# Keys and queries of a hybrid layer's mixer as one wide seven-product projection, with the mixer's steps in another order

## The chip, the cores and the metric

The kernel runs on one core of a Trainium2 chip. The metric is the device time of one execution in microseconds (us). TensorE multiplies, VectorE (DVE) and ScalarE (ACT) prepare its operands and empty its accumulators in PSUM, GpSimd (POOL) does a little elementwise work and issues some transfers, SyncE (SP) issues the transfers of the weights.

## The reference

One layer of a hybrid decoder on 256 tokens of width 2048, all in float32: a half feed-forward block, a mixer, a second half feed-forward block, a final norm.

```python
def rmsnorm(x, g):
    return x * rsqrt(mean(x * x, -1) + EPS) * g

def layer(h):
    h = h + 0.5 * swiglu(rmsnorm(h, ffn1_norm), ffn1_w_in, ffn1_w_out)
    u = rmsnorm(h, mix_norm) @ w_in_mix        # columns: pool 1024 | q 512 | k 512 | v 1024 | gate 1024 | rank 16
    y_pool = pool_mixer(u[..., :1024], w_pool, pool_scale)
    y_gla = gla_mixer(q, k, v, gate, rank, w_alpha, b_alpha, gla_norm)
    h = h + concat([y_pool, y_gla], -1) @ w_out_mix
    h = h + 0.5 * swiglu(rmsnorm(h, ffn2_norm), ffn2_w_in, ffn2_w_out)
    return rmsnorm(h, final_norm)

def swiglu(h, w_in, w_out):                    # w_in: 2048 x 11264, w_out: 5632 x 2048
    gate, up = split(h @ w_in, 2, -1)
    return (silu(gate) * up) @ w_out
```

The pooling mixer takes means over the last 2, 4, 8 or 16 tokens (four groups of 256 channels), minus the token, through a 256x256 matrix for each group. The other one is gated linear attention with four heads in chunks of 64 tokens: the decay is the log-sigmoid of `rank @ w_alpha + b_alpha`, divided by 16 and summed along the chunk; keys and queries are scaled by its exponentials; the output of each head is normalised by its own root mean square and multiplied by silu of the gate columns.

## The kernel before

Tokens are two row tiles of 128 (`t`). Activations are kept transposed, 16 k-tiles of 128 channels by 256 tokens, split into a high and a low part (`hT1`); they are TensorE's stationary operand. Weights stream past them, up to 512 columns to a matmul. Each product is made of three matmuls, high by high, low by high and high by low (`three`, L198 to L202), so almost every matmul in the trace has line L202.

**Weights.** `load` (L142) brings 128 x 2048 numbers through SP's queue into one of a few raw buffers. ScalarE rounds them to the high part (L166), VectorE subtracts that to get the low part (L167). The results lie in a ring of blocks of 512 columns (16 blocks, six more in the feed-forward stages). The blocks are taken in turn; where a run of blocks crosses the ring's end, its split is cut in two.

**Two kinds of step.** A step covers two k-tiles (a pair, `kp`) by 1024 columns. A plain step (S, `s_step`) is 8 products, 24 matmuls, from four ring blocks. A seven-product step (W, `w_step`, after Strassen and Winograd) is 21 matmuls, from seven blocks. For it VectorE also takes differences of the raw weights (`less`, L190) and makes four sums of the activations for each pair (`s_factors`, L416, L442, and the split L153/L154). Four of the seven products go into four PSUM banks of their own (`pw`), which `combine` (L326 to L330) adds up at the end of a group. `Group` keeps a group of steps in PSUM; `wide` runs one in the mixer, with hooks called after given steps. `W_MIX` lists the pairs that are W steps in the mixer.

**PSUM and SBUF.** The pool `psy` has two buffers of two banks, `ps_t` has four banks, for `pw` and everything small. In SBUF the dictionary `homes` gives a name to each place of the mixer; names that share a place follow one another.

**Order of the mixer.** `finish1` ends FFN 1, and between its transposes runs the first halves of two `project` calls: the last 336 gate columns with 16 rank columns (`w_mgr`), and the keys (`w_mk`). Then come the rest of these two, the rank rows (`r_sb`, transposed to `rT`, L799 to L802), the values `mv` (a wide group, steps SSWWWWSS, with `decay` as a hook: `z`, L817, its Abs, Exp and Ln, `la`, L824, and the exponentials `E1`, `E2`, `Es`), `keys`, the queries `mq` (`project`), the pooling columns `mp` (wide, with `state` and `scores` as hooks), `attend` (o, its squares `sq_o`, the roots `ro_r` through POOL at L366, the scalings L962), `pool(0)` and gate columns `mg0`, `pool(1)` and `mg1`, then the output projection `h2` in two halves, in which `gate_y` multiplies y by the gates and transposes it (`tp_y`). The sums of `h2` with `h_mid`, loaded by POOL's queue, are at L1086; the instructions of the first sums are kept in `cleared`.

Each engine runs its instructions in one fixed order, and a waiting instruction holds back all behind it on its engine. A scheduler lays these orders out when the program is built, from the data flow and its own costs; it may move an instruction across steps where its operands allow. `issue_after` binds it: what its block issues on the engine of the named instruction comes behind that instruction there, in order only, without a wait for its end.

Of the kernel before, what the change touches and what calls it, by code (L numbers as in the profile page):

```python
# [28 lines left out]
F32 = mybir.dt.float32  # L29
# [54 lines left out]
W_MIX = (0, 1, 2, 3)  # L84
# [4 lines left out]
def layer(ctx: ExitStack, tc: tile.TileContext, io):  # L89
# [94 lines left out]
    def w_step(src):  # L184
# [11 lines left out]
        f.update(zip(("T1", "T3", "T2", "T4"), parts_of(w, PAIRS)))  # L196
# [503 lines left out]

    kd = list(range(KD))
    hact = act_of(*hT1)
    early = []

    def finish1(np_, grp, h):
# [27 lines left out]
    ps_r, ps_k = early  # L733
# [75 lines left out]
    E1 = block([P, HEADS, T], F32, "E1")  # L809
    E2 = gpool.tile([P, HEADS, T], F32, tag="g_lo", name="E2")  # L810
    Es = gpool.tile([P, HEADS * DK], F32, tag="g_lo", name="Es")

    def decay(_):
        z = []
        for t in range(NT):
# [3 lines left out]
            z.append(zt)  # L819
# [454 lines left out]
```

## Time and profile before

| | before |
|---|---|
| median of 3 runs | 1695.22 us (1694.63 to 1695.98) |
| profiled execution, its own time | 1695.91 us |
| its span (first to last instruction) | 1694.1 us, granted clock 0.998 |
| VectorE busy, share of the span | 1517.9 us, 90% |
| ScalarE busy, share of the span | 1028.1 us, 61% |
| mixer: first matmul of `mgr` | 702.9 us |
| mixer: first transpose of y | 908.9 us |

In lines of the profile an operation stands as output<-inputs, with names of the program without their numbers; "128x512" is partitions by elements. In a timeline, the first number is the start from the beginning of the span, the second the duration, both in us. In a group line, "x32 | 12.7, 396 | 0.0" is the count, the busy time in us, the mean of one in ns, and the engine's idle time before them with what ended it.

### The profile page before, as it was taken

What the parts mean: (1) busy time and instruction counts of PE and PEld (TensorE: products, weight loads), DVE (VectorE), ACT (ScalarE), POOL (GpSimd) and SP (SyncE); (2) the same over time, 40 slices, a digit from 0 to 9 for tenths busy, and PEclk for the clock granted to TensorE, in tenths of its full rate; (3) what the DMA queues carried; (4) which work ended last, traced back from release to release, by engine and by line L of the source; (5) the groups of instructions that cost most, each with busy time, mean ns of one, the idle gap of its engine ahead of it and who ended that gap; (6) DMA issues with size and microseconds to landing.
All of it is one profiled execution on the core that took longest, in us unless ns stands there. A gap on an engine that the chain in (4) does not pass through costs nothing.

```text
span 1694.1 us, 20977 instructions
## 1 busy us (share of the span) xinstructions
PE 1678.6 (99%) x7654; PEld 1392.0 (82%) x7654; DVE 1517.9 (90%) x1709; ACT 1028.1 (61%) x1309; POOL 58.1 (3%) x69
## 2 busy tenths in 40 slices
PE   9999999999999999999999999999999999999997
PEld 6888888888888888887898888888888888888876
DVE  8899999999999996777867888999999999999987
ACT  7665665665665664557565665656656656656554
POOL 0000000000000000000000000000000000000001
PEclk9999999999999999999999999999999999999999
DMA  9766766866866777546466584666767667677772
GB/s 344 281 183 234 247 185 230 257 170 228 261 183 219 257 213 252 211 140 229 166 208 204 169 318 141 205 232 201 214 229 226 207 225 227 196 235 227 218 275 75
DMA packets 106330, 369.50 MB, mean 218 GB/s; under 512 B 11873, under 2 KB 15073, under 8 KB 106226
## 3 DMA queue, kind: packets, MB, share of 16 engines
q1 hardware_dynamic: 97026, 335.63, 58.4%
q0 software_dynamic: 8480, 31.46, 8.7%
q8 instruction: 60, 0.98, 0.2%
q10 hardware_dynamic: 720, 1.07, 0.2%
q14 instruction: 44, 0.36, 0.1%
HBM read 340.85 MB, written 27.26 MB: 217 GB/s over the span
## 4 chain that ended last, share of the span: by engine, by line
PE 90%; DVE 5%; DMA 3%; issue 2%; ACT 1%; SPq 0%; ACTq 0%; DVEq 0%
PE ps_zi L202 15%; PE ps_fi L202 15%; PE ps_zo L202 14%; PE ps_fo L202 13%; PE pw_zi L202 8%; PE pw_fi L202 8%; PE ps_h L202 3%; DVE ring_lo L167 3%; PE ps_mg L202 2%; PE ps_mp L202 2%; PE ps_mv L202 2%; DMA ring_raw<-in_ffn_w_in 2%; PE pw L202 1%; PE ps_w_mk L202 1%; PE ps_mq L202 1%
## 5 line engine op out<-in xcount | busy, mean ns | idle before, releaser
L166 ACT CAST ring_hi<-ring_raw 128x1024 fp32r<-128x1024 f32 (+2 forms) x947 | 843.0, 930 | 525.3 <-DMA ring_raw<-in_ffn_w_in 109.8
L167 DVE TENSOR_TENSOR ring_lo<-ring_raw,ring_hi 128x1024 fp32r<-128x1024 f32 (+5 forms) x797 | 969.2, 1244 | 112.1 <-ACT ring_hi L166 110.9
L190 DVE TENSOR_TENSOR ring_raw<-ring_raw 128x1024 f32<-128x1024 f32 (+1 forms) x381 | 324.3, 863 | 2.6 <-DMA ring_raw<-in_ffn_w_in 2.1
L202 PE MATMUL ps_fi<-ring_hi,xT_hi 128*128 128x512 f32 x368 | 141.4, 390 | 2.4 <-ACT ring_hi L166 2.4
L202 PE MATMUL ps_fi<-ring_lo,xT_hi 128*128 128x512 f32 x368 | 143.4, 390 | 0.2 <-DVE ring_lo L167 0.2
L202 PE MATMUL ps_fi<-ring_hi,xT_lo 128*128 128x512 f32 x368 | 143.2, 389 | 0.0
L202 PE MATMUL ps_zi<-ring_lo,h_hi 128*128 128x512 f32 x362 | 141.2, 390 | 0.1
L202 PE MATMUL ps_zi<-ring_hi,h_lo 128*128 128x512 f32 x362 | 139.7, 390 | 0.0
L202 PE MATMUL ps_zi<-ring_hi,h_hi 128*128 128x512 f32 x362 | 139.4, 390 | 0.0
L202 PE MATMUL ps_fo<-ring_lo,fhi 128*128 128x512 f32 x352 | 138.2, 393 | 0.3 <-DVE ring_lo L167 0.3
L202 PE MATMUL ps_fo<-ring_hi,flo 128*128 128x512 f32 x352 | 137.8, 391 | 0.0
L202 PE MATMUL ps_fo<-ring_hi,fhi 128*128 128x512 f32 x352 | 135.9, 391 | 0.0
L202 PE MATMUL ps_zo<-ring_lo,zhi 128*128 128x512 f32 x338 | 131.9, 390 | 1.2 <-DVE ring_lo L167 1.2
L202 PE MATMUL ps_zo<-ring_hi,zlo 128*128 128x512 f32 x338 | 131.7, 391 | 0.0
L202 PE MATMUL ps_zo<-ring_hi,zhi 128*128 128x512 f32 x338 | 131.6, 394 | 0.0
L202 PE MATMUL pw_zi<-ring_hi,s_z 128*128 128x512 f32 x342 | 117.6, 389 | 0.1
L202 PE MATMUL pw_fi<-ring_hi,s_f 128*128 128x512 f32 x336 | 116.1, 390 | 0.3 <-ACT ring_hi L166 0.3
L202 PEld LDWEIGHTS ps_fi<-ring_hi,xT_hi 128*128 128x128 f32 x368 | 69.0, 188 | 17.5 <-ACT ring_hi L166 3.4
L202 PEld LDWEIGHTS ps_fi<-ring_lo,xT_hi 128*128 128x128 f32 x368 | 69.1, 188 | 15.1 <-DVE ring_lo L167 0.8
L202 PEld LDWEIGHTS ps_fi<-ring_hi,xT_lo 128*128 128x128 f32 x368 | 69.1, 188 | 14.3
L202 PEld LDWEIGHTS ps_zi<-ring_lo,h_hi 128*128 128x128 f32 x362 | 68.0, 188 | 14.5 <-DVE ring_lo L167 0.6
L202 PEld LDWEIGHTS ps_zi<-ring_hi,h_hi 128*128 128x128 f32 x362 | 68.0, 188 | 14.1
(353 smaller groups left out, 2597.1 us busy)
## 6 DMA issues: line engine op xcount, KB each, us to landing
ring_raw<-in_ffn_w_in SPq DMA_DIRECT2D x350, 512.0 KB, 5.4
ring_raw<-in_ffn_w_out SPq DMA_DIRECT2D x176, 512.0 KB, 5.7
ring_raw<-in_w_out_mix SPq DMA_DIRECT2D x32, 512.0 KB, 4.9
hd<-half_f POOLq DMA_DIRECT2D x18, 512.0 KB, 8.4
hd<-half_z POOLq DMA_DIRECT2D x18, 512.0 KB, 7.8
ring_raw<-in_w_mv SPq DMA_DIRECT2D x16, 512.0 KB, 4.3
ring_raw<-in_w_mp SPq DMA_DIRECT2D x16, 512.0 KB, 4.9
ring_raw<-in_w_mg SPq DMA_DIRECT2D x16, 352.0 KB, 3.5
```

Of the source, the lines that this page charges most:

```text
L166: nc.scalar.copy(out=hi[:, j:k, :], in_=src[:, i + j : i + k, :])
L167: nc.vector.tensor_tensor(out=lo, in0=src[:, i : i + n, :], in1=hi.bitcast(F32), op=ALU.subtract)
L190: nc.vector.tensor_tensor(out=out, in0=x, in1=y, op=ALU.subtract)
L202: nc.tensor.matmul(ps, x, y, start=start and i == 0, stop=stop and i == 2, **kw)
```

## The change

Keys and queries become one wide group, `mkq`, of 1024 columns (`w_mkq` holds both), in pair order 0, 1, 2, 5, 3, 4, 6, 7, with W steps for pairs 4, 5 and 6. Its first two steps stand in `finish1`, where the first halves of the two projections stood. `W_MIX` is now the pairs 4 to 7, for all three wide groups. The order behind it is new: the whole of `mgr`, the pooling columns `mp` (hooks after its second step: `turn_r` and `decay`), `mg0` in two halves with `decay2` and `heads_in` (keys and queries turned and scaled), the values `mv` (hook: `scores`), `state` and `pool(0)`, and `mg1`, with `attend` and `pool(1)` after its first half; `load_h(0)` and `load_h(1)` follow. `decay` is cut in two, and `la` is now a minimum for each row tile and one subtraction for both. High and low parts of the pooling weights, `band`, `v` and `up` have other homes. Four places order instructions of W steps: behind `made_r` (the rank rows), step 2 of `mp`; behind `cleared[0]`, the low parts of step 2, and behind `cleared[1]`, step 3, both in the second half of `h2`, where step 3 stood behind `cleared[0]`.

```diff
-W_MIX = (0, 1, 2, 3)
+W_MIX = (4, 5, 6, 7)
...
-    def w_step(src):
+    def w_step(src, behind=None):
...
-        f.update(zip(("T1", "T3", "T2", "T4"), parts_of(w, PAIRS)))
+        with tc.issue_after(behind) if behind else nullcontext():
+            f.update(zip(("T1", "T3", "T2", "T4"), parts_of(w, PAIRS)))
...
+    def wide_group(name, order, w_kps, adds):
+        kinds = "".join("W" if kp in w_kps else "S" for kp in order)
+        return Group({"y": psy}, ("y",), kinds, name, ones=four_banks, adds=adds, calm=True)
...
-    early = []
+    heads = []
+    heads_order = (0, 1, 2, 5, 3, 4, 6, 7)
...
             if np_ == 1:
-                w, cw = (("w_mgr", 336), ("w_mk", CW))[n % 2]
-                early.append(project(hact, kd, io[w], cw, w, part=slice(0, KD // 2)))
+                if not heads:
+                    heads.append(wide_group("mkq", heads_order, (4, 5, 6), lambda: heads_adds))
+                kp = heads_order[n % 2]
+                heads[0].s(half_steps(hact, kp), s_step(io["w_mkq"][kp]))
             transposed_rows(
...
-    def wide(act, src, order, w_kps, s_in, name, adds, hooks={}, behind={}):
...
+    def wide(act, src, order, w_kps, s_in, name, adds, hooks={}, grp=None, behind={}, low_behind={}):
+        grp = grp or wide_group(name, order, w_kps, lambda: adds)
+        kinds = grp.kinds
         for i, kp in enumerate(order):
+            if i < grp.n:
+                continue
             if kinds[i] == "W":
                 with tc.issue_after(behind[i]) if i in behind else nullcontext():
-                    b = w_step(src[kp])
+                    b = w_step(src[kp], low_behind.get(i))
                 grp.w(half_steps(act, kp), s_in[kp], b)
             else:
                 grp.s(half_steps(act, kp), s_step(src[kp]))
...
+    h_make = s_factors(pair_of(*hT1), W_MIX, "mix", (("h", "h0"), ("h", "h1")))
+    h_in = {kp: h_make(kp) for kp in W_MIX}
...
+    heads_adds = [block([P, 2, CW], F32, f"mkq_add{t}") for t in range(NT)]
...
-    gw = (352, 352, 336 - RANK)
-    ps = project(hact, kd, io["w_mgr"], gw[2] + RANK, "mgr", ps_r, slice(KD // 2, KD))
+    grp = wide(hact, io["w_mkq"], heads_order, (4, 5, 6), h_in, "mkq", None, grp=heads[0])
+    out_of(grp, kq)
+    k_sb, q_sb = ([kq[t][:, n * CW : (n + 1) * CW] for t in range(NT)] for n in range(2))
+    ps = project(hact, kd, io["w_mgr"], gw[2] + RANK, "mgr")
...
+    r_sb = small.tile([P, NT, RANK], F32, tag="r_sb", name="r_sb")
     for t in range(NT):
-        r_sb = small.tile([P, RANK], F32, tag="r_sb", name=f"r_sb{t}")
-        nc.vector.tensor_scalar_mul(r_sb, ps[t][:, gw[2] : gw[2] + RANK], rs(t))
-        tp = ps_t.tile([P, CW], F32, tag="tp", name=f"tp_r{t}")
-        nc.tensor.transpose(tp[:RANK, :P], r_sb, ident)
-        nc.vector.tensor_copy(rT[:RANK, t * P : (t + 1) * P], tp[:RANK, :P])
+        made_r = nc.vector.tensor_scalar_mul(r_sb[:, t, :], ps[t][:, gw[2] : gw[2] + RANK], rs(t)).ins
         nc.scalar.activation(
             out=gsil[t][:, gw[0] + gw[1] :], in_=ps[t][:, : gw[2]], func=AF.Silu, scale=rs(t)
         )
...
+    z = []
+    def turn_r(_):
+        tp = ps_t.tile([P, CW], F32, tag="tp", name="tp_r")
+        for t in range(NT):
+            nc.tensor.transpose(tp[:RANK, t * P : (t + 1) * P], r_sb[:, t, :], ident)
+        nc.vector.tensor_copy(rT[:RANK, :], tp[:RANK, :T])
     def decay(_):
-        z = []
         for t in range(NT):
             zt = ps_t.tile([P, CW], F32, tag="tp", name=f"z{t}")
             nc.tensor.matmul(zt, rT[:, t * P : (t + 1) * P], walpha, start=True, stop=True)
             nc.scalar.activation(out=e[:, t, :], in_=zt, func=AF.Abs)
-            z.append(zt)
+            nc.vector.tensor_scalar(
+                out=la[:, t, :], in0=zt, scalar1=0.0, scalar2=None, op0=ALU.min
+            )
         nc.scalar.activation(out=e, in_=e, func=AF.Exp, scale=-1.0)
         nc.scalar.activation(out=e, in_=e, func=AF.Ln, bias=1.0)
-        for t in range(NT):
-            nc.vector.scalar_tensor_tensor(
-                out=la[:, t, :], in0=z[t], scalar=0.0, in1=e[:, t, :], op0=ALU.min, op1=ALU.subtract
-            )
+        nc.vector.tensor_tensor(out=la, in0=la, in1=e, op=ALU.subtract)
+    def decay2(_):
@@ -844,11 +879,7 @@
         nc.scalar.activation(out=Es, in_=sf, func=AF.Exp)
-    ps = project(hact, kd, io["w_mk"], CW, "mk", ps_k, slice(KD // 2, KD))
-    k_sb = gpool.tile([P, NT, HEADS * DK], F32, tag="g_hi", name="k_sb")
...
         for s, tp in headsT(k_sb, "k"):
             nc.vector.tensor_tensor(out=kiT[:, s, :], in0=tp, in1=E2[:, s, :], op=ALU.mult)
...
-    mix_order = [kp for kp in range(KD // 2) if kp not in W_MIX]
-    mix_order = mix_order[:2] + list(W_MIX) + mix_order[2:]
...
+    mix_order = (0, 1, 4, 5, 6, 7, 2, 3)
+    pool_order = (0, 1, 4, 5, 2, 6, 7, 3)
+    def gate_cols(c, hooks={}):
+        c0 = c * gw[0]
+        ps = None
+        for i in range(2):
+            ps = project(hact, kd, io["w_mg"][c], gw[c], f"mg{c}", ps, slice(i * KD // 2, (i + 1) * KD // 2))
+            if i in hooks:
+                hooks[i](None)
...
+    adds = [block([P, 2, CW], F32, f"mp_add{t}") for t in range(NT)]
+    out_of(wide(hact, io["w_mp"], pool_order, W_MIX, h_in, "mp", adds, behind={2: made_r}, hooks={1: lambda _: (turn_r(None), decay(None))}), up)
+    def heads_in(_):
+        keys()
...
-    out_of(wide(hact, io["w_mv"], mix_order, W_MIX, h_in, "mv", adds, {5: decay}), v)
-    keys()
-    ps = project(hact, kd, io["w_mq"], CW, "mq")
-    q_sb = gpool.tile([P, NT, HEADS * DK], F32, tag="g_lo", name="q_sb")
...
-    for s, tp in headsT(q_sb, "q"):
...
+    gate_cols(0, {0: decay2, 1: heads_in})
...
-    adds = [block([P, 2, CW], F32, f"mp_add{t}") for t in range(NT)]
-    grp = wide(hact, io["w_mp"], mix_order, W_MIX, h_in, "mp", adds, {0: state, 5: scores})
-    up = hpool.tile([P, NT, 2 * CW], F32, tag="h1", name="up")
...
-    out_of(grp, up)
-    attend(None)
+    v = hpool.tile([P, NT, HEADS * DV], F32, tag="h1", name="v")
...
+    adds = [block([P, 2, CW], F32, f"mv_add{t}") for t in range(NT)]
+    out_of(wide(hact, io["w_mv"], mix_order, W_MIX, h_in, "mv", adds, {6: scores}), v)
...
-    load_h(0)
...
-        wp_hi, wp_lo = (block([P, 2, 2, DV], F32R, f"wp_{x}{i}") for x in ("hi", "lo"))
+        if True:
+            both = hpool.tile([P, 2, 2 * CW], F32R, tag="h0", name=f"wp{i}s")
+            wp_hi, wp_lo = (both[:, x].rearrange("p (j c d) -> p j c d", j=2, c=2) for x in range(2))
         split_to(wp_hi, wp_lo, wp)
...
-    for c in range(2):
-        pool(c)
-        c0 = c * gw[0]
-        ps = project(hact, kd, io["w_mg"][c], gw[c], f"mg{c}")
...
+    (state(None), pool(0))
+    gate_cols(1, {0: lambda _: (attend(None), pool(1))})
+    load_h(0)
     load_h(1)
...
-        grp = wide(yact, io["w_out_mix"][np_], out_order[np_], W_OUT if np_ else (), y_in, f"h2{np_}", adds, hooks[np_], behind={3: cleared[0]} if np_ else {})
+        grp = wide(yact, io["w_out_mix"][np_], out_order[np_], W_OUT if np_ else (), y_in, f"h2{np_}", adds, hooks[np_], behind={3: cleared[1]} if np_ else {}, low_behind={2: cleared[0]} if np_ else {})
```

What this does to the order of instructions shows at three places. On TensorE, before, in the value projection (`ps_mv`, `pw`) at the first matmul of `decay`:

```order
L202 MATMUL pw_5419<-ring_lo,s_mix_5321 128x512
L202 MATMUL pw_5419<-ring_hi,s_mix_5321 128x512
L817 MATMUL z_5549<-walpha,rT 128x512
L202 MATMUL pw_5418<-ring_lo,s_mix_5321 128x512
L202 MATMUL pw_5418<-ring_hi,s_mix_5321 128x512
```

And after, in the pooling projection (`ps_mp`):

```order
L203 MATMUL ps_mp_5486<-ring_hi,s_mix_5094 128x512
L203 MATMUL ps_mp_5486<-ring_hi,h_hi_127 128x512
L851 MATMUL z_5552<-walpha,rT 128x512
L851 MATMUL z_5556<-walpha,rT 128x512
L203 MATMUL pw_5576<-ring_hi,h_hi_127 128x512
```

Before, the second of the two stood 53 rows further on; now they are neighbours.

On VectorE, at the end of the last chunk of FFN 2's first product, before (`add_zi` are the combining sums, `ps_zi` the sum with the plain part, `ring_lo` splits of weights):

```order
L327 TENSOR_TENSOR add_zi_1_11575<-pw_zi_0_11377,add_zi_0_11574 128x512
L328 TENSOR_TENSOR add_zi_0_11574<-pw_zi_1_11378,add_zi_1_11575 128x512
L329 TENSOR_TENSOR add_zi_1_11575<-pw_zi_1_11378,add_zi_1_11575 128x512
L519 TENSOR_TENSOR ps_zi_0_11362<-ps_zi_0_11362,add_zi_0_11574 128x1024
L167 TENSOR_TENSOR ring_lo<-ring_raw,ring_hi 128x2048
L330 TENSOR_TENSOR add_zi_1_11575<-pw_zi_1_11378,add_zi_1_11575 128x512
L167 TENSOR_TENSOR ring_lo<-ring_raw,ring_hi 128x2048
```

And after:

```order
L167 TENSOR_TENSOR ring_lo<-ring_raw,ring_hi 128x1024
L328 TENSOR_TENSOR add_zi_1_11598<-pw_zi_0_11400,add_zi_0_11597 128x512
L167 TENSOR_TENSOR ring_lo<-ring_raw,ring_hi 128x2048
L329 TENSOR_TENSOR add_zi_0_11597<-pw_zi_1_11401,add_zi_1_11598 128x512
L330 TENSOR_TENSOR add_zi_1_11598<-pw_zi_1_11401,add_zi_1_11598 128x512
L167 TENSOR_TENSOR ring_lo<-ring_raw,ring_hi 128x2048
L520 TENSOR_TENSOR ps_zi_0_11385<-ps_zi_0_11385,add_zi_0_11597 128x1024
L167 TENSOR_TENSOR ring_lo<-ring_raw,ring_hi 128x1024
L331 TENSOR_TENSOR add_zi_1_11598<-pw_zi_1_11401,add_zi_1_11598 128x512
```

The same five sums now have splits between them, one of them ahead of the second sum and one ahead of the 1024-wide one.

On ScalarE, from the last square of the first row tile's o to the scalings of the second one's, before (`ring_hi` casts here are gate weights, `wp_hi` pooling weights):

```order
L379 ACTIVATE sq_o_6116,so_6103<-o_1_6107 128x256
L166 CAST ring_hi<-ring_raw 128x2x352
L962 ACTIVATE y_g_hi<-o_0_6104,ro_r 128x256 x2
L962 ACTIVATE y_g_hi<-o_1_6107,ro_r 128x256 x2
L379 ACTIVATE sq_o_6143,so_6132<-o_0_6133 128x256
L379 ACTIVATE sq_o_6145,so_6132<-o_0_6133 128x256
L379 ACTIVATE sq_o_6147,so_6132<-o_1_6138 128x256
L153 CAST wp_hi_6172<-wp_6167 128x1024
L379 ACTIVATE sq_o_6149,so_6132<-o_1_6138 128x256
L166 CAST ring_hi<-ring_raw 128x2x352 x3
L962 ACTIVATE y_g_lo<-o_0_6133,ro_r 128x256 x2
```

And after, from the split of the pooling weights to the scalings of the second row tile (`ring_hi` casts are output weights, `p_hi` the pooled rows, `gsil` the gates):

```order
L153 CAST wp1s<-wp_6441 128x1024
L380 ACTIVATE sq_o_6419,so_6408<-o_0_6409 128x256
L380 ACTIVATE sq_o_6421,so_6408<-o_0_6409 128x256
L166 CAST ring_hi<-ring_raw 128x1024
L380 ACTIVATE sq_o_6423,so_6408<-o_1_6414 128x256
L380 ACTIVATE sq_o_6425,so_6408<-o_1_6414 128x256
L153 CAST p_hi_6451<-pp_0_6453 128x512
L166 CAST ring_hi<-ring_raw 128x512
L914 ACTIVATE gsil_5140<-ps_mg_6318,r_h_r 128x352
L914 ACTIVATE gsil_5141<-ps_mg_6318,r_h_r 128x352
L988 ACTIVATE y_g_lo<-o_0_6409,ro_r 128x256 x2
```

The squares and scalings of the attention now share ScalarE's queue with the pooling of `pool(1)`, the last gates and the first output weights.

More of the change, by code (lines that the diff above doesn't have):

```diff
@@ L699, in project, with four_banks, half_steps, a @@
         return ps
+    def four_banks():
+        return [ps_t.tile([P, CW], F32, tag="tp", name=f"pw_{i}") for i in range(4)]
+    def half_steps(act, kp):
+        def a(t, k):
+            hi, lo = act(2 * kp + k)
+            return hi[:, t * P : (t + 1) * P], lo[:, t * P : (t + 1) * P]
+        return a
+    def wide_group(name, order, w_kps, adds):
+        kinds = "".join("W" if kp in w_kps else "S" for kp in order)
+        return Group({"y": psy}, ("y",), kinds, name, ones=four_banks, adds=adds, calm=True)
     kd = list(range(KD))
     hact = act_of(*hT1)
-    early = []
+    heads = []
+    heads_order = (0, 1, 2, 5, 3, 4, 6, 7)
     def finish1(np_, grp, h):
@@ L808, in layer @@
     e = gpool.tile([P, NT, HEADS * DK], F32, tag="g_hi", name="e")
-    E1 = block([P, HEADS, T], F32, "E1")
     E2 = gpool.tile([P, HEADS, T], F32, tag="g_lo", name="E2")
     Es = gpool.tile([P, HEADS * DK], F32, tag="g_lo", name="Es")
+    z = []
+    def turn_r(_):
+        tp = ps_t.tile([P, CW], F32, tag="tp", name="tp_r")
+        for t in range(NT):
+            nc.tensor.transpose(tp[:RANK, t * P : (t + 1) * P], r_sb[:, t, :], ident)
+        nc.vector.tensor_copy(rT[:RANK, :], tp[:RANK, :T])
     def decay(_):
-        z = []
         for t in range(NT):
@@ L859, in headsT @@
                     nc.tensor.transpose(
-                        tp[:, j, t * P : (t + 1) * P], src[:, t, hh * DK : (hh + 1) * DK], ident
+                        tp[:, j, t * P : (t + 1) * P], src[t][:, hh * DK : (hh + 1) * DK], ident
                     )
@@ L875, in layer @@
-    mix_order = mix_order[:2] + list(W_MIX) + mix_order[2:]
-    v = [block([P, HEADS * DV], F32, f"v{t}") for t in range(NT)]
-    def out_of(grp, to):
+    mix_order = (0, 1, 4, 5, 6, 7, 2, 3)
[7 more added lines that the diff above has]
+                hooks[i](None)
@@ L880, in out_of @@
         for t in range(NT):
             nc.scalar.activation(
-                out=to[t], in_=grp.acc[t].rearrange("p n c -> p (n c)"), func=AF.Copy, scale=rs(t)
+                out=gsil[t][:, c0 : c0 + gw[c]], in_=ps[t][:, : gw[c]], func=AF.Silu, scale=rs(t)
             )
-        for t in range(NT):
+    adds = [block([P, 2, CW], F32, f"mp_add{t}") for t in range(NT)]
+    out_of(wide(hact, io["w_mp"], pool_order, W_MIX, h_in, "mp", adds, behind={2: made_r}, hooks={1: lambda _: (turn_r(None), decay(None))}), up)
@@ L885, in out_of @@
+    def heads_in(_):
+        keys()
+        for s, tp in headsT(q_sb, "q"):
             nc.vector.scalar_tensor_tensor(
-                out=to[t], in0=grp.add[t].rearrange("p n c -> p (n c)"), scalar=rs(t), in1=to[t],
-                op0=ALU.mult, op1=ALU.add,
-            )
-    adds = [block([P, 2, CW], F32, f"mv_add{t}") for t in range(NT)]
-    out_of(wide(hact, io["w_mv"], mix_order, W_MIX, h_in, "mv", adds, {5: decay}), v)
-    keys()
-    ps = project(hact, kd, io["w_mq"], CW, "mq")
@@ L895, in layer @@
-    q_sb = gpool.tile([P, NT, HEADS * DK], F32, tag="g_lo", name="q_sb")
-    for t in range(NT):
-        nc.scalar.activation(out=q_sb[:, t, :], in_=ps[t], func=AF.Copy, scale=rs(t))
-    qdT = block([P, HEADS, T], F32, "qdT")
-    for s, tp in headsT(q_sb, "q"):
-        nc.vector.scalar_tensor_tensor(
-            out=qdT[:, s, :], in0=tp, scalar=DK**-0.5, in1=E1[:, s, :], op0=ALU.mult, op1=ALU.mult
-        )
+                out=qdT[:, s, :], in0=tp, scalar=DK**-0.5, in1=E1[:, s, :], op0=ALU.mult, op1=ALU.mult
+            )
@@ L1023, in pool @@
                 )
-    for c in range(2):
-        pool(c)
-        c0 = c * gw[0]
-        ps = project(hact, kd, io["w_mg"][c], gw[c], f"mg{c}")
-        for t in range(NT):
-            nc.scalar.activation(
-                out=gsil[t][:, c0 : c0 + gw[c]], in_=ps[t][:, : gw[c]], func=AF.Silu, scale=rs(t)
-            )
+    (state(None), pool(0))
+    gate_cols(1, {0: lambda _: (attend(None), pool(1))})
+    load_h(0)
     load_h(1)
@@ L1246 @@
         "w_mgr": quads(wm[:, O_G + 2 * gw :]),
[L1247 to L1248 removed]
+        "w_mkq": steps(wm[:, None, O_K : O_K + CW], wm[:, None, O_Q : O_Q + CW])[0],
         "w_mg": np.stack([quads(wm[:, O_G + c * gw : O_G + (c + 1) * gw]) for c in range(2)]),
```

42 lines of the change are left out of this document (19 added, 23 removed).

## The prediction

> **What bounds the kernel now.** I read the page's first part, then the waits of TensorE, then windows of 20 to 50 us over the mixer. The page gives busy time, share and instructions by engine, and the granted TensorE clock in tenths for 40 slices.
>
> ```profile
> PE 1678.6 (99%) x7654; PEld 1392.0 (82%) x7654; DVE 1517.9 (90%) x1709; ACT 1028.1 (61%) x1309; POOL 58.1 (3%) x69
> PEclk9999999999999999999999999999999999999999
> ```
>
> TensorE works for 99% of the span, with an even clock. Its waits, in us, times, longest:
>
> ```profile
> PE ps_fi L202 <- ACT ring_hi L166: 2.4, 2, 1.6
> ...
> PE ps_fi L202 <- DVE ring_lo L167: 0.2, 1, 0.2
> ```
>
> Six rows, from 2.4 down to 0.2, and none in the mixer. In the mixer TensorE has no gap (columns: window, its length, then busy time of PE, PEld, DVE, ACT):
>
> ```profile
> 700.00:740.00 40.00, 40.00 (x217) 35.66 (x216) 34.06 (x60) 26.02 (x41) 2.39 (x2) 1.00 0.61 207
> 860.00:900.00 40.00, 40.00 (x262) 39.58 (x261) 24.41 (x42) 25.01 (x45) 3.38 (x3) 1.00 0.61 200
> ```
>
> So two things can move the time: how many columns TensorE streams, and whether VectorE or ScalarE, moved by the new order, makes it wait. VectorE has 5.9 of 40 us to spare where the key projection stands, and 15.6 where the attention ends.
>
> **Fewer matmuls.** Keys and queries were two projections of 96 matmuls (three rows of x32 each, one of each here):
>
> ```profile
> L202 PE MATMUL ps_w_mk<-ring_hi,h_hi 128*128 128x512 f32 x32 | 12.7, 396 | 0.0
> L202 PE MATMUL ps_mq<-ring_hi,h_hi 128*128 128x512 f32 x32 | 12.6, 392 | 0.0
> ```
>
> Afterwards they are five steps of 24 and three of 21: 183 for 192, nine fewer. Matmuls overlap, so the price is the distance of starts, here of 512-column ones:
>
> ```profile
> 1628.21 0.39 PE L202 MATMUL ps_zi<-ring_hi,h_hi 128*128 128x512 f32 x1
> ...
> 1628.89 0.39 PE L202 MATMUL ps_zo<-ring_hi,zhi 128*128 128x512 f32 x1
> 1630.45 0.50 PE L202 MATMUL ps_zo<-ring_lo,zhi 128*128 128x512 f32 x1 [1.17 <-DVE ring_lo L167]
> 1630.79 0.39 PE L202 MATMUL ps_zo<-ring_hi,zlo 128*128 128x512 f32 x1
> ```
>
> From 1628.21 to 1628.89 are three steps of 0.227 us. Nine of them are 9 x 0.227 = **-2.04 us**. All other counts of columns stay.
>
> The Trainium skill (TensorE: Matmul & The Clock Gate, section "Wait — 56ns, not 53.3ns?") puts matmuls back to back at the columns over 2.4 GHz plus 2.5 ns, 215.8 ns for 512. By that the nine would be 1.94 us; the trace's 0.227 decides.
>
> **The wait at 1629.** The same rows show TensorE's one wait behind the mixer: 1630.45 - 1628.89 - 0.227 = 1.3 us, which the profile calls 1.17. VectorE then:
>
> ```profile
> 1626.98 1.22 DVE L519 TENSOR_TENSOR ps_zi<-ps_zi,add_zi 128x1024 f32<-128x1024 f32 x1
> 1628.12 2.28 DVE L167 TENSOR_TENSOR ring_lo<-ring_raw,ring_hi 128x2048 fp32r<-128x2048 f32 x1
> 1630.32 0.68 DVE L330 TENSOR_TENSOR add_zi<-pw_zi,add_zi 128x512 f32<-128x512 f32 x1
> ```
>
> The split that TensorE needs starts at 1628.12, behind the output sums of the chunk, and takes 2.28. A seven-product step takes seven blocks of the ring, a plain one four, so the three new ones turn the ring by nine blocks, and the splits of FFN 2 are cut elsewhere. In the new order a 2048 split stands ahead of the last three sums, another ahead of L520, and so those blocks come earlier by up to 2 x 0.68 + 1.22 = 2.6 us, which covers 1.2. I count **-1.2**. Ends: +1 (the sums, now late, hold up the next) and -1.3. Where the order alone says that a wait goes, its inputs may be late too, so I give the whole gain two chances in three.
>
> **Rank rows.** Before, the two matmuls of `decay` stand alone between 512-column ones, 13 us apart:
>
> ```profile
> 782.28 0.39 PE L202 MATMUL ps_mv<-ring_hi,h_hi 128*128 128x512 f32 x1
> 782.60 1.12 PE L817 MATMUL z<-walpha,rT 17*128 17x512 f32 x2
> 783.65 0.50 PE L202 MATMUL ps_mv<-ring_lo,h_hi 128*128 128x512 f32 x1
> ```
>
> From 782.28 to 783.65 is 1.37, of which 0.227 is the plain matmul, so one (two records) costs 1.14 with its entry and exit. Side by side one exit and one entry go; I take about a quarter of that: **-0.3** (0 to -0.6).
>
> **VectorE beside keys and queries.** Its prices (count, busy us, mean ns):
>
> ```profile
> L167 DVE TENSOR_TENSOR ring_lo<-ring_raw,ring_hi 128x1024 fp32r<-128x1024 f32 x60 | 72.3, 1221 | 14.5 <-ACT ring_hi L166 14.2
> L167 DVE TENSOR_TENSOR ring_lo<-ring_raw,ring_hi 128x2048 fp32r<-128x2048 f32 x29 | 66.3, 2291 | 23.4 <-ACT ring_hi L166 23.4
> L190 DVE TENSOR_TENSOR ring_raw<-ring_raw 128x512 f32<-128x512 f32 x24 | 16.5, 686 | 0.2
> L190 DVE TENSOR_TENSOR ring_raw<-ring_raw 128x1024 f32<-128x1024 f32 x12 | 14.6, 1220 | 0.2
> L167 DVE TENSOR_TENSOR ring_lo<-ring_raw,ring_hi 128x512 fp32r<-128x512 f32 x15 | 10.2, 687 | 2.8 <-ACT ring_hi L166 2.8
> L154 DVE TENSOR_TENSOR s_mix<-sf_mix,s_mix 128x512 fp32r<-128x512 f32 x4 | 2.7, 684 | 0.0
> L416 DVE TENSOR_TENSOR sf_mix<-sa_mix 128x128 f32<-128x128 f32 x8 | 2.0, 286 | 0.0
> ```
>
> A plain step is one split, 2.29. A seven-product one is differences of 1.22 + 2 x 0.69 and splits of 0.69 + 3 x 1.22, together 6.95. After FFN 1, three of each are 27.7. The activation sums of four pairs, which stood beside the value projection, come here: 4 x (2 x 0.68 + 4 x 0.29) = 10.1. With four combining sums of 0.69 it is 40.5 us of VectorE for some 40 us in which TensorE runs through these products and into the gate columns. That is full. I walked the new order against these durations: the first sums are needed at 725.0 on the clock of before and ready at 724.0, the low parts 2 us ahead, the last blocks 0.9 us. I take 0; the bound above is a split late at each of the three steps, 3 x 1.22 = 3.7. Less than 0 it cannot be, as TensorE does not wait there now.
>
> **The subtraction behind Exp and Ln.** `la` is now two minima straight from PSUM and one 1024-wide subtraction in VectorE's queue, which waits about 2.5 us for ScalarE; queued behind it are the splits of the next two seven-product steps of the pool projection, with 0.5 to 1.7 us to spare by the same walk. ScalarE around it before:
>
> ```profile
> 784.42 1.05 ACT L166 CAST ring_hi<-ring_raw 128x1024 fp32r<-128x1024 f32 x1
> 785.49 1.28 ACT L821 ACT_TABLE_LOAD   x1
> 786.78 1.06 ACT L821 ACTIVATE e<-e 128x1024 f32<-128x1024 f32 x1
> ```
>
> The load stands flush between its neighbours: 1.28, and nothing more. I take 0.
>
> **The end of the attention.** `attend` moves from ahead of both gate pieces into the middle of the second, which shortens the cover. What TensorE waits for behind it is ScalarE's scaling of o, and last y's transposes:
>
> ```profile
> 859.86 0.20 ACT L379 ACTIVATION_READ_ACCUMULATOR sq_o<-o 128x1 f32 x1
> ...
> 863.11 1.57 ACT L962 ACTIVATE y_g_hi<-o,ro_r 128x256 f32<-128x256 f32 x4 [1.24 <-DVE ro_r L374]
> ```
>
> ```profile
> 908.86 0.38 PE L460 MATMUL tp_y<-ident,y_g_hi 128*128 128x128 f32 x2
> ```
>
> From the last square (860.06) to the scalings, through VectorE and POOL, are 3.05 us, and 1.57 for themselves. The first scalings end at 864.68, so TensorE has 44 us of other work up to tp_y. In the new order 45 matmuls of 512 columns (10.2 us) and 28 of 128 to 352 (at about 0.11, by width) stand between the last o and tp_y: 13 us. The o matmuls of the second row tile need the banks which these scalings free, and ring casts stand behind the scalings. By the walk, margins here are 0.2 to 1.8 us at six places: some will be missed. I take **+1.0** (0 to 2). The loads that move are cheap:
>
> ```profile
> h_mid<-hd POOLq DMA_DIRECT2D x2, 1024.0 KB, 7.1
> wp<-in_w_pool SPq DMA_DIRECT2D x4, 256.0 KB, 2.9
> ```
>
> `h_mid` is read by the sums of the output projection, 192 x 0.227 = 43.6 us after its first matmul; uncovered it would be 7.1. The pool weights on SP now come behind some output weights in its queue; a late one costs up to 2.9, which lies inside the next rival. The edges on `made_r` and `cleared` hold splits behind short VectorE sums that run anyway; they order, and add no work: 0, and up to one 0.68 sum each.
>
> **Sum.** -2.04 - 1.2 - 0.3 + 1.0 = -2.5 on the profiled execution, 1695.91, so 1693.4. That execution is 0.69 over the median of 1695.22, so **1692.7**. A measurement of this kernel can tell 0.2%, 3.4 us, from no change.
>
> **The rivals.**
>
> *It gains more.* All small waits of the mixer close. TensorE has four late starts of 0.2 to 0.4 us from 820 to 998, the last here:
>
> ```profile
> 997.22 0.39 PE L202 MATMUL ps_zi<-ring_hi,h_hi 128*128 128x512 f32 x1
> 997.74 0.50 PE L202 MATMUL ps_zi<-ring_lo,h_hi 128*128 128x512 f32 x1
> 998.08 0.39 PE L202 MATMUL ps_zi<-ring_hi,h_lo 128*128 128x512 f32 x1
> ```
>
> From 997.22 to 998.08 are two steps and 0.41. Together 1.1. Without my +1.0 it is -3.5 - 1.1 = -4.6: 1690.6. For it: TensorE stands at 99%, margins were positive everywhere. Against: the margins are thin, and all must hold.
>
> *Nine products gone, and nothing seen.* VectorE is late by one split at each new step, 3.7: -3.5 + 3.7 = +0.2, 1695.4. For it speaks the 40.5 us of work, against it the ring of 16 blocks, which lets splits run ahead.
>
> *Slower: the roots of the attention uncovered.* ScalarE runs in order. Both times that it stands for ro_r, 3.05 us, with a VectorE split of 1.22 ahead of the root, TensorE has used up the casts made before: 2 x (3.05 + 1.22) = 8.5, so -3.5 + 8.5 = +5.0: 1700.2. It decides over 6.9 us of lost time, by when cover of 13 us is gone. For it: cover falls from 44 to 13. Against: VectorE has 15.6 of 40 us idle there now, and 13 is twice the chain.
>
> *Table loads longer than the row.* If something as long as a load, 1.28, stood behind each of the two ahead of Ln, the subtraction would come 2.6 later and eat 0.5 to 1.7 of margin: a wait of 0.9 to 2.1, about 1.5. -2.5 + 1.5 = -1.0: 1694.2. The Trainium skill (ScalarE: Activation LUTs, section "What ACT_TABLE_LOAD costs") says this: 1283 ns, and 1380 ns of drain at every switch, by which it would be 2.8. The rows agree on the load, and contradict the drain.
>
> **How the numbers follow.** Chances: forecast, with -1.0 to -3.4, 0.50; more 0.27; nothing seen 0.10; slower 0.09; table loads 0.04. Faster by over 0.2% is the second alone, 0.27; slower the fourth, 0.09; the rest, 0.64, is same. For 8 in 10 the range takes in the forecast's own (1691.8 to 1694.2), most of the second, and the third down to its price: 1690.5 to 1695.4.
>
> **What would show it.** Right: 183 matmuls of keys and queries in about 41.5 us, no wait of ps_zo at the end of FFN 2's last chunk, rank rows side by side, TensorE at 99%, and waits of under 1 us around tp_y. Wrong: a wait of ps_mkq or pw on ring_lo or s_mix over 1 us (VectorE full), of o or ps_h on ring_hi or y_g_hi over 3 us (roots), or ps_zo still waiting.

## The result, and the profile after

The changed kernel takes 1704.47 us (median of six runs, 1703.61 to 1706.53) against 1695.6 before on the same chip: ratio 1.0053, 95% interval 1.004 to 1.0066. It is slower by 8.9 us, where 1692.7 was forecast and 1695.4 was the range's upper end. The profiled execution has a span of 1702.3 us.

First the page's first part and clock, then all of TensorE's waits (total us, times, longest), of the changed kernel:

```profile
PE 1689.3 (99%) x7645; PEld 1391.5 (82%) x7645; DVE 1534.7 (90%) x1730; ACT 1035.3 (61%) x1315; POOL 59.4 (3%) x69
PEclk9999999999999999999999999999999999999999
```

```profile
PE idle L631 <- DVE zeros L626: 1.2, 1, 1.2
PE ps_fi L203 <- ACT ring_hi L166: 1.2, 2, 1.0
PE pw L203 <- DVE h_lo L356: 0.5, 1, 0.5
PE ps_fi L203 <- DVE ring_lo L167: 0.2, 1, 0.2
```

This is an odd picture. Nine matmuls are gone, the waits add up to 3.1 us where they were 5.6, the clock is as even as before, and yet TensorE is busy for 1689.3 us instead of 1678.6. Almost nothing waits; the matmuls follow one another more slowly. Where? The tiles' views give the first and last start of each stage's matmuls: FFN 1 from the first `ps_fi` to the last `ps_fo`, the mixer to the first `ps_zi`, FFN 2 to the last `ps_zo`. They are taken from the profiled execution, the time is the median.

| | time, us | FFN 1 | mixer | FFN 2 |
|---|---|---|---|---|
| before | 1695.6 | 696.3 | 288.7 | 690.1 |
| changed | 1704.5 | 701.9 | 287.2 | 694.7 |

The mixer, which the change rewrote, is 1.5 us shorter. FFN 1, whose instructions stand on every engine in the same order as before up to its last transposes, is 5.6 us longer. That is more than executions differ by: in the seven kernels below that have these same instructions and no slowing, FFN 1 takes 694.4 to 697.5. The change reached a stage in which it changed nothing. A window in FFN 1 shows it in the count of matmuls that start in 100 us. Before, and then changed (window, its length, PE busy and count, clock, DMA):

```profile
100.00:200.00 100.00, 99.71 (x448) 1.00 0.68 209
200.00:300.00 100.00, 100.00 (x450) 1.00 0.72 225
300.00:400.00 100.00, 100.00 (x447) 1.00 0.74 234
```

```profile
100.00:200.00 100.00, 100.00 (x446) 1.00 0.69 212
200.00:300.00 100.00, 100.00 (x446) 1.00 0.69 219
300.00:400.00 100.00, 100.00 (x441) 1.00 0.73 232
```

1345 matmuls became 1333, 0.9% fewer, at a full clock and 100% busy. In the timeline of TensorE, changed kernel, every second matmul of a stretch is late by some 10 ns:

```profile
327.31 0.40 PE L203 MATMUL ps_fi<-ring_hi,xT_hi 128*128 128x512 f32 x1
327.55 0.39 PE L203 MATMUL ps_fi<-ring_lo,xT_hi 128*128 128x512 f32 x1
327.77 0.40 PE L203 MATMUL ps_fi<-ring_hi,xT_lo 128*128 128x512 f32 x1
328.01 0.39 PE L203 MATMUL ps_fi<-ring_hi,xT_hi 128*128 128x512 f32 x1
328.24 0.40 PE L203 MATMUL ps_fi<-ring_lo,xT_hi 128*128 128x512 f32 x1
328.48 0.39 PE L203 MATMUL ps_fi<-ring_hi,xT_lo 128*128 128x512 f32 x1
328.71 0.40 PE L203 MATMUL ps_fi<-ring_hi,xT_hi 128*128 128x512 f32 x1
```

From 327.31 to 328.71 are six steps of 0.233 us; it was 0.227. The mean over all starts of 512-column matmuls that follow one another between 100 and 680 us is 0.2269 before (2469 of them) and 0.2295 changed (2450).

What can differ in FFN 1, if not the instructions? The places of its tiles. `r_sb` became one tile for both row tiles, 128 bytes per partition instead of 64, in the pool `small` with two buffers. So `small` grew by 128 bytes, and every tile behind it moved by 128: in FFN 1 the sums, the extra raw buffer, the six extra ring blocks, one third of the activation sums. In the built kernel the extra high blocks begin at 194592 instead of 194464. All large tiles ahead of them begin at 160 past a multiple of 256, and so did these; now they begin at 32 past one. What is left of such a place after the multiples of 256 is called its offset modulo 256 here. Sorting the 512-column matmuls of the trace by the offset modulo 256 of what they and their two neighbours read, streamed or stationary: where all agree 0.2279 us (1412), where they don't 0.2316 (1038).

### The profile page after: what moved, and what is told of

It is laid out like the page before. It is cut to its first block, busy times and chain, and to the rows that moved or that the text cites. A ratio compares the mean times of both kernels' runs of the same rounds, so it can differ in the third digit from the quotient of the medians.

```text
span 1702.3 us, 21017 instructions
## 1 busy us (share of the span) xinstructions
PE 1689.3 (99%) x7645; PEld 1391.5 (82%) x7645; DVE 1534.7 (90%) x1730; ACT 1035.3 (61%) x1315; POOL 59.4 (3%) x69
## 4 chain that ended last, share of the span: by engine, by line
PE 97%; DVE 1%; DMA 1%; issue 0%; SPq 0%; ACT 0%; DVEq 0%; POOLq 0%; POOL 0%
PE ps_zi L203 17%; PE ps_fi L203 16%; PE ps_fo L203 14%; PE ps_zo L203 14%; PE pw_zi L203 9%; PE pw_fi L203 9%; PE ps_h L203 3%; PE pw L203 2%; PE ps_mkq L203 2%; PE ps_mg L203 2%; PE ps_mv L203 2%; PE ps_mp L203 2%; PE ps_mgr L203 1%; DVE ring_lo L167 1%; PE ztp L536 1%; PE ftp L536 1%
## 5 line engine op out<-in xcount | busy, mean ns | idle before, releaser
L167 DVE TENSOR_TENSOR ring_lo<-ring_raw,ring_hi 128x1024 fp32r<-128x1024 f32 (+4 forms) x803 | 974.4, 1241 | 105.0 <-ACT ring_hi L166 104.2
L190 DVE TENSOR_TENSOR ring_raw<-ring_raw 128x512 f32<-128x512 f32 (+1 forms) x390 | 331.3, 861 | 2.5 <-DMA ring_raw<-in_ffn_w_in 2.1
L203 PEld LDWEIGHTS ps_zi<-ring_hi,h_lo 128*128 128x128 f32 x362 | 68.0, 188 | 14.9
```

The lines of the kernel that those rows point to most:

```text
L167: nc.vector.tensor_tensor(out=lo, in0=src[:, i : i + n, :], in1=hi.bitcast(F32), op=ALU.subtract)
L190: nc.vector.tensor_tensor(out=out, in0=x, in1=y, op=ALU.subtract)
L203: nc.tensor.matmul(ps, x, y, start=start and i == 0, stop=stop and i == 2, **kw)
```

## The experiments

Theory A: the 128 bytes slow TensorE. Theory B: the new stream of instructions does. The first nine kernels differ from the one that they come from only in places of tiles; their instructions and the order on every engine are those of that kernel.

**The shift taken out of the changed kernel.**

```diff
-    small = ctx.enter_context(tc.tile_pool(name="small", bufs=2))
+    small = ctx.enter_context(tc.tile_pool(name="small", bufs=2)); small.tile([P, 16], F32, tag="pad", name="pad")
...
-    tri = mixc.tile([P, 2, P], F32, name="tri")
+    r_sb, tri = (mixc.tile(x, F32, name=n) for x, n in (([P, NT, RANK], "r_sb"), ([P, 2, P], "tri")))
...
-    r_sb = small.tile([P, NT, RANK], F32, tag="r_sb", name="r_sb")
```

> The changed kernel with the same instructions in the same order; only the places of the feed-forward tiles (extra ring blocks, extra raw buffer, sums) go back by 128 bytes, to where they were in the kernel before, by 128 bytes of padding behind the small tiles and r_sb at the head of the mixer's own tiles. Theory A (128 bytes of shift slow TensorE): the distance of starts of 512-column matmuls in FFN 1 falls from 0.2293 back to 0.2270 us, and the time is 1692 to 1694, faster than before by 1.5 to 3.5 us. Theory B (the new instruction stream as such makes all of TensorE slower): still 1704.

Measured: 1691.19 us, ratio 0.9974 (0.9964 to 0.9985) to before, which was 1695.8 in these runs. The mean start distance in FFN 1 is 0.2269 again. TensorE's busy time, on the page's first part:

```profile
PE 1675.3 (99%) x7645; PEld 1391.1 (82%) x7645; DVE 1532.8 (91%) x1730; ACT 1035.1 (61%) x1315; POOL 59.3 (4%) x69
```

14.0 us of busy time go with no instruction changed. Theory B is out. The change without its shift is faster than the kernel before by 4.6 us (2.5 to 6.1 by the interval), a little more than the 1.5 to 3.5 expected.

**The shift put into the kernel before.**

```diff
-    small = ctx.enter_context(tc.tile_pool(name="small", bufs=2))
+    small = ctx.enter_context(tc.tile_pool(name="small", bufs=2)); small.tile([P, 16], F32, tag="pad", name="pad")
```

> The kernel before with the same instructions in the same order; 128 bytes of padding behind the small tiles move the feed-forward tiles as in the changed kernel. Theory A: starts of 512-column matmuls 0.2293 us apart in FFN 1 instead of 0.2270, some 6900 of them, so 10 to 14 us slower: 1705 to 1710. Theory B: 1695.5, no change.

Measured: 1709.98, ratio 1.0082 (1.0067 to 1.0097). FFN 1 takes 703.6, FFN 2 696.6, the mixer 289.6. An unused tile of 128 bytes costs 14.2 us.

**All tiles shifted together.**

```diff
-    const = ctx.enter_context(tc.tile_pool(name="const", bufs=1))
+    const = ctx.enter_context(tc.tile_pool(name="const", bufs=1)); const.tile([P, 32], F32, name="pad")
```

> The kernel before with 128 bytes of padding ahead of all larger tiles, so that all of them move by 128 bytes and keep their distances. Theory A1 (what counts is that operands read together stand at different offsets within some block of memory): no change, 1695.5. Theory A2 (what counts is the absolute place: operands at 32 bytes past a multiple of 256 are slow, at 160 past it are not): every matmul is slow as those of the shifted blocks were in the changed kernel, 0.2323 for 0.2270 us, so 6900 x 0.0053 = 37 us slower, 1732.

Measured: 1695.05, ratio 0.9995 (0.9986 to 1.0004), mean distance 0.2269. Here every large tile begins at 32 past a multiple of 256, as the slow ones did in the changed kernel. It isn't the place, it is the distance between places: A1 holds, A2 is out.

**256 bytes instead of 128** (the changed kernel with the padding of the second run):

> The changed kernel with 128 bytes more of padding behind the small tiles: the feed-forward tiles stand 256 bytes from where they were before. If the slowing repeats every 256 bytes, the time is as in the kernel with the shift taken out, 1692 to 1694. If only multiples of 512 or 1024 are good, it stays at about 1704. Theory B: 1704.

Measured: 1691.0, ratio 0.997 (0.9959 to 0.9981). The slowing repeats every 256 bytes. The time is a little under the 1692 to 1694 expected. Which two accesses disturb each other, the next runs asked.

**Only the activations off**, 128 bytes of padding ahead of them and 128 behind them:

```diff
-    const = ctx.enter_context(tc.tile_pool(name="const", bufs=1))
+    const = ctx.enter_context(tc.tile_pool(name="const", bufs=1)); const.tile([P, 32], F32, name="pad")
...
-    units = ctx.enter_context(tc.tile_pool(name="units", bufs=1))
+    units = ctx.enter_context(tc.tile_pool(name="units", bufs=1)); units.tile([P, 32], F32, name="pad1")
```

> The kernel before, same instructions, same order; only the activations (most of TensorE's stationary operands) stand 128 bytes off, all weights, sums and other tiles keep their distances (multiples of 256). Theory P (TensorE's two own reads, the streamed operand and the stationary one, disturb each other when their offsets modulo 256 differ): nearly every 512-column matmul is slow, 0.2323 for 0.2270 us, 1725 to 1735. Theory Q (the streamed operand is disturbed by what VectorE and ScalarE read and write meanwhile): almost no change, 1695 to 1699.

Measured: 1729.61, ratio 1.0203 (1.0188 to 1.0218), mean distance 0.2325. The windows of this run, beside those above:

```profile
100.00:200.00 100.00, 100.00 (x440) 1.00 0.69 206
200.00:300.00 100.00, 100.00 (x440) 1.00 0.68 221
300.00:400.00 100.00, 100.00 (x436) 1.00 0.73 226
```

1316 for 1345, 2.2% fewer, and the waits of TensorE add up to 2.4 us. Theory P holds: what counts is whether what is streamed and what is loaded as the stationary operand begin at the same offset modulo 256. Among themselves, the weights' raw numbers, high parts and low parts stand as before here. The other engines don't cause it in this trace: between 100 and 680 us, starts with operands at two offsets are 0.2326 us apart beside an idle ScalarE (615 of them) and 0.2329 beside a busy one (1599); beside an idle VectorE they are 0.2335 (92), beside a busy one 0.2328 (2122). The Trainium skill (TensorE: Matmul & The Clock Gate, section "Step-by-step: what each phase is for") gives the two operands a read port each and says that loading the next weights takes no read bandwidth from the running matmul. The trace contradicts that at unequal offsets, 0.2325 for 0.2269. At equal ones it is not tested, as every matmul timed here has a load of its own.

**Only the extra ring blocks off**, and **all but them off** (the second with the padding of `small` as well):

```diff
         if n_blocks:
-            blocks.extend(
-                *(pool.tile([P, n_blocks, CW], F32R, name=f"{name}_{x}") for x in ("hi", "lo"))
-            )
+            pads = [pool.tile([P, 32], F32, name=f"{name}_pad0")] if pool is not units else []; two = [pool.tile([P, n_blocks, CW], F32R, name=f"{name}_{x}") for x in ("hi", "lo")]
+            pads += [pool.tile([P, 32], F32, name=f"{name}_pad1")] if pool is not units else []
+            blocks.extend(*two)
```

> The kernel before, same instructions, same order; of the feed-forward tiles only the six extra ring blocks stand 128 bytes off, the sums and the extra raw buffer are in place. Theory P: the matmuls that stream these blocks (27% of those in FFN) are slow against the activations, so most of the 14 us: 1704 to 1710. If the sums and the raw buffer do the harm: 1695 to 1698.

> The counterpart: sums, extra raw buffer and all the mixer's own tiles stand 128 bytes off, the six extra ring blocks are in place. Theory P: only the few matmuls whose stationary operand lies there (8%) are slow: 1697 to 1700. If the sums and the raw buffer do the harm: 1704 to 1710.

Measured: 1706.37, ratio 1.0066 (1.0051 to 1.0081), and 1699.86, ratio 1.0027 (1.0017 to 1.0038). The parts, 10.8 and 4.3 us, add up to 15.1, about the 14.2 of both together; the blocks are 72% of it. In the first of the two runs the matmuls with operands at two offsets have a mean distance of 0.2325 again (665 between 100 and 680 us).

**64 bytes instead of 128** (the padding in `small` half as wide, `[P, 8]`):

> The kernel before, same instructions, same order, with the feed-forward and mixer tiles 64 bytes off instead of 128. If what counts is which half of 256 bytes an operand begins in, 64 bytes on from 160 is 224 and still in the same half: no change, 1695.5. If every offset but a multiple of 256 is slow: 1703 to 1710.

Measured: 1708.08, ratio 1.0078 (1.0061 to 1.0095). It is no matter of halves: 64 bytes are about as bad as 128.

**Only the raw weights off**, which TensorE doesn't read (padding ahead of the three main raw buffers and behind them):

> The kernel before, same instructions, same order; the three main buffers of raw weights, which DMA writes and ScalarE and VectorE read and TensorE never touches, stand 128 bytes off, all else on one offset modulo 256. If only TensorE's own two reads disturb each other: 1695.5. If reads of VectorE and ScalarE at another offset disturb TensorE too (in the changed kernel a quarter of the matmuls with both operands in place were slow beside a VectorE split that reads shifted tiles): 1698 to 1705.

Measured: 1695.21, ratio 0.9999 (0.999 to 1.0009). What VectorE, ScalarE and the transfers read and write in these buffers at another offset costs TensorE nothing that this run shows.

Three more kernels took the forecast's other terms apart. **The order edges taken out** of the changed kernel with 256 bytes of shift:

```diff
-    out_of(wide(hact, io["w_mp"], pool_order, W_MIX, h_in, "mp", adds, behind={2: made_r}, hooks={1: lambda _: (turn_r(None), decay(None))}), up)
+    out_of(wide(hact, io["w_mp"], pool_order, W_MIX, h_in, "mp", adds, hooks={1: lambda _: (turn_r(None), decay(None))}), up)
...
-        grp = wide(..., behind={3: cleared[1]} if np_ else {}, low_behind={2: cleared[0]} if np_ else {})
+        grp = wide(..., behind={3: cleared[0]} if np_ else {})
```

> The changed kernel with all tiles on one offset modulo 256 (as in the run with 256 bytes of shift, 1691.0), and its four order edges taken out: nothing is placed behind made_r and cleared, step 3 of the output projection stands behind cleared[0] as in the kernel before. By the prediction's step (the edges order, and add nothing): 1690.5 to 1692. Rival (the edges are what closes the mixer's small waits): 1693 to 1695.

Measured: 1699.96, ratio 1.0029 (1.0018 to 1.004) to before: 9.0 us slower than the same kernel with them (9.7, if each is compared with the kernel before on its own chip). That lies outside both times expected. TensorE's waits in it, the largest five:

```profile
PE ps_zo L203 <- DVE ring_lo L167: 2.4, 3, 0.9
PE ps_h L203 <- DVE h_mid L1104: 1.6, 1, 1.6
PE idle L631 <- DVE zeros L626: 1.2, 1, 1.2
PE tp_r L845 <- DVE r_sb L830: 1.2, 1, 1.2
PE ps_zi L203 <- DVE h_mid L1104: 1.0, 1, 1.0
...
```

Two of them, of `tp_r` and `ps_h`, are for results that an edge puts first (rank rows and the first output sums); that of `ps_zi` is for a last output sum. Those of `ps_zo` lie in FFN 2, where no edge stands. But the scheduler laid FFN 2 out anew as well: of its 3095 matmuls 2574 keep their order among each other, of VectorE's some 650 instructions there 443. TensorE and VectorE at the sums of the output projection, in this kernel:

```profile
946.77 0.39 PE L203 MATMUL ps_h<-ring_hi,y_lo 128*128 128x512 f32 x1
948.77 0.47 PE L203 MATMUL ps_h<-ring_hi,y_hi 128*128 128x512 f32 x1 [1.61 <-DVE h_mid L1104]
```

```profile
944.93 1.23 DVE L167 TENSOR_TENSOR ring_lo<-ring_raw,ring_hi 128x1024 fp32r<-128x1024 f32 x1 [1.02 <-ACT ring_hi L166]
946.08 1.41 DVE L190 TENSOR_TENSOR ring_raw<-ring_raw 128x512 f32<-128x512 f32 x2
947.40 1.22 DVE L1104 TENSOR_TENSOR h_mid<-ps_h,h_mid 128x1024 f32<-128x1024 f32 x1
```

TensorE needs the PSUM banks that the sum of 1.22 us frees; VectorE had a split ahead of it, which waited for its cast for 1.02, and then two differences. The sum began flush behind these, with no wait of its own. With the edges, VectorE is there first and waits for TensorE:

```profile
942.37 1.23 DVE L1104 TENSOR_TENSOR h_mid<-ps_h,h_mid 128x1024 f32<-128x1024 f32 x1 [0.87 <-PE ps_h L203]
```

The mixer takes 292.2 us without the edges for 286.3 with them, FFN 2 691.3 for 687.8. So some 5.8 us are lost where the edges stand, and 3.5 in FFN 2, in another order of its instructions.

**The ring turned by nine blocks** in the kernel before (one line more ahead of the mixer's `project`: `blocks.skip(9)`):

> The kernel before with nine blocks of the weight ring skipped at the start of the mixer, so that FFN 2's splits are cut as in the changed kernel (VectorE's splits into the low parts there: 93 of 512 columns, 165 of 1024, 1 of 1536, 49 of 2048). Theory (the wait at 1629 comes from the cut): it goes, 1694.3, and up to 1 us more from smaller waits in FFN 2. Rival (it comes from elsewhere): 1695.5, the wait of ps_zo stays at 1.2.

Measured: 1697.15, ratio 1.001 (1.0001 to 1.0018). That is neither of the two times expected, but slower by 2.1, with FFN 2 at 692.7 for 690.1. The wait did not go; it moved to an earlier chunk:

```profile
1505.45 0.39 PE L202 MATMUL ps_zo<-ring_hi,zhi 128*128 128x512 f32 x1
1507.04 0.50 PE L202 MATMUL ps_zo<-ring_lo,zhi 128*128 128x512 f32 x1 [1.20 <-DVE ring_lo L167]
```

```profile
1503.57 1.22 DVE L519 TENSOR_TENSOR ps_zi<-ps_zi,add_zi 128x1024 f32<-128x1024 f32 x1
1504.70 2.28 DVE L167 TENSOR_TENSOR ring_lo<-ring_raw,ring_hi 128x2048 fp32r<-128x2048 f32 x1
```

It is the same pattern, the 2048 split right behind the chunk's sum. The cut alone does not take the wait away. Why FFN 2 is 2.6 longer, the run does not show.

**Keys and queries in plain steps**, in the changed kernel with 256 bytes of shift:

```diff
-                    heads.append(wide_group("mkq", heads_order, (4, 5, 6), lambda: heads_adds))
+                    heads.append(wide_group("mkq", heads_order, (), lambda: heads_adds))
...
-    grp = wide(hact, io["w_mkq"], heads_order, (4, 5, 6), h_in, "mkq", None, grp=heads[0])
+    grp = wide(hact, io["w_mkq"], heads_order, (), h_in, "mkq", None, grp=heads[0]); blocks.skip(9)
```

> The changed kernel with all tiles on one offset modulo 256 (1691.0), and keys and queries in eight plain steps: nine more 512-column matmuls, no differences, no combining sums for them; nine ring blocks are skipped behind them so that all later splits are cut alike. By the prediction's step (TensorE is the bound and each costs 0.227): 1693.0. Rival (VectorE, relieved of 14 us of work, gives it back): 1691.0 to 1691.5.

Measured: 1694.44 us (1691.19 to 1697.66, a wide spread), ratio 0.9996 (0.9987 to 1.0005) to before, 3.4 over the kernel with the three steps (4.15, if each is compared with the kernel before on its own chip), where 2.0 was expected. The stage tells it better: the mixer takes 288.9 for 286.3, 2.6 us, for nine matmuls at 2.04. VectorE, busy 38.77 of the 40 us from 700 with the three steps, is busy 29.79 without:

```profile
700.00:740.00 40.00, 29.79 (x51) 1.00 0.56 197
```

Nine us less of VectorE's work gave nothing back: it had run beside TensorE's, which did not wait for it.

## Why the prediction was wrong

The step that failed is in "Fewer matmuls": "All other counts of columns stay", and with it the price of 0.227 us, which the forecast took for all of them as given. The counts did stay. The price did not: in the changed kernel more than a quarter of the FFN's 512-column matmuls read operands at two offsets modulo 256, and the mean over both FFNs rose to 0.2295. That term was missing from the sum. It measures 1704.47 - 1691.0 = 13.5 us by the run with 256 bytes of shift, 13.3 by the run that takes the shift out, 14.2 in the kernel before. The diff had it in plain sight, in one line: `r_sb` with twice the bytes, in a pool that lies ahead of the FFN's tiles. None of the five cases contained it, so none came near; the case that was slower named the roots of the attention, and TensorE had no wait for them.

The terms of the sum can be judged in the two runs without the shift, whose instructions are those of the changed kernel:

- **Nine matmuls, -2.04, and the rank rows, -0.3: right.** The mixer falls from 288.7 to 286.4 and 286.3, about 2.3 us. The rank rows stand side by side, as here in the changed kernel:

```profile
778.30 0.39 PE L203 MATMUL ps_mp<-ring_hi,h_hi 128*128 128x512 f32 x1
778.62 1.98 PE L851 MATMUL z<-walpha,rT 17*128 17x512 f32 x4
780.53 0.50 PE L203 MATMUL pw<-ring_hi,h_hi 128*128 128x512 f32 x1
```

  From 778.30 to 780.53 is 2.23, without the plain matmul 2.00; two apart cost 2 x 1.14 = 2.28.
- **VectorE full beside keys and queries, but in time: right.** It is busy 37.34 of 40 us there (34.06 before), and TensorE has no wait of `ps_mkq`.

```profile
700.00:740.00 40.00, 40.00 (x186) 33.15 (x185) 37.34 (x68) 25.07 (x44) 1.87 (x2) 1.00 0.46 149
```

- **The subtraction behind Exp and Ln: right.** VectorE waited 1.68 us (2.5 by the walk), and TensorE did not. The table loads again stand flush, so that rival is out.

```profile
788.04 1.23 DVE L859 TENSOR_TENSOR la<-la,e 128x1024 f32<-128x1024 f32 x1 [1.68 <-ACT e L858]
```

```profile
781.70 1.05 ACT L166 CAST ring_hi<-ring_raw 128x1024 fp32r<-128x1024 f32 x1
782.77 1.28 ACT L857 ACT_TABLE_LOAD   x1
784.06 1.06 ACT L857 ACTIVATE e<-e 128x1024 f32<-128x1024 f32 x1
785.03 0.61 ACT L166 CAST ring_hi<-ring_raw 128x512 fp32r<-128x512 f32 x1
785.65 1.28 ACT L858 ACT_TABLE_LOAD   x1
786.95 1.06 ACT L858 ACTIVATE e<-e 128x1024 f32<-128x1024 f32 x1
```

- **The end of the attention, +1.0: too careful.** No wait of o or tp_y. The one new wait in the mixer is 0.5 us (0.6 in the two runs), of `pw` for the transposed rows in the second half of the output projection.
- **The wait at 1629, -1.2: not borne out by the cut, and its size not shown.** In the changed kernel it is gone, and with 256 bytes of shift too. With the shift taken out, the same instructions in the same order wait 0.7 us there, and turning the ring in the kernel before moved it to 1505. So cut and order do not settle it; that the moment at which sums and 2048 splits fall decides it is argued, not shown. FFN 2 shortened by 1.1 and 2.3 us in the two runs, but kernels with the instructions of before and no slowing already differ by 1.8 there (688.6 to 690.4).
- **The edges, 0: wrong.** The schedule made without them is 9.0 us slower, 5.8 of that in the mixer.

Without the shift the change is worth 4.6 and 4.8 us (together 2.5 to 7.0 by the intervals), nearest to the first rival's 4.6. That is luck in part. The mixer's 2.3 are the nine matmuls and the rank rows and leave nothing for the small waits that this rival closes. Of the rest, 2.5 and 0.6 us lie ahead of the change, in FFN 1 and its start (waits for first casts of 2.4 us before, 0.3 and 1.1 in these two), and shouldn't be counted to it.

## What to carry to other kernels

When a diff changes a tile's size or moves it to another pool, list where every later tile of every stage comes to lie, and compare the offsets modulo 256 of what TensorE streams and what it loads; a stage that the diff doesn't touch may pay. If a stage is slower with TensorE at 99% busy, no waits and a full clock, compare the distances of its matmuls' starts before looking for a wait; busy time hides it. And an order edge that costs nothing by itself may be what an order rests on: price it by what would stand there without it, and remember that taking it out can lay out later stages anew.

## What the runs showed of the hardware

TensorE's matmul of 512 columns with its own stationary load starts every 0.2269 us in the kernel before, where both operands begin at the same offset modulo 256 bytes of a partition, and every 0.2325 us, 2.5% later, in the run where nearly all of them don't. That is shown for 128 bytes; with part of the tiles off, 64 bytes cost the whole kernel 12.5 us, 128 bytes 14.2, and 256 bytes nothing. Absolute places don't matter (1695.05 us with all tiles 128 bytes on), nor does the offset of the raw weights, which only VectorE, ScalarE and DMA touch (1695.21). What in the chip makes two such reads disturb each other is not shown.

Open: with the extra blocks off, matmuls with both operands in place were slower too, 0.2279 for 0.2269. Most of that is an after-effect. Sorted by their distance from the last matmul with operands at two offsets, the first three behind it are 0.2308 apart (273 of them), the fourth to tenth 0.2278 (488), the later ones 0.2272 (1022). Of the later ones, those beside a ScalarE cast into a shifted block have 0.2281 (166), those with no shifted access of ScalarE or VectorE to the ring or the raw weights beside them 0.2269 (587). So such writes may cost something as well. A run that shifts what is written and not what TensorE reads wasn't made, so this is argued, not shown.
